# A decoder step on one Trainium2 core: the scan's first product, inverse and value transposes and the norms' sums in whole 128x128 tiles

## The chip, the core and the metric

The kernel runs on one core of a Trainium2 chip. The core has a matrix engine (TensorE, PE in the profile; PEld is its weight load), a vector engine (DVE), a scalar engine (ACT), GpSimd (POOL) and an engine that issues transfers (SyncE, SP), each with its own instruction stream. The metric is the device time of one execution, in microseconds (us), median of several runs. Everything below is 32-bit floating point.

## The reference

Two decoder layers run on 512 prompt tokens and 8 x 4 sample tokens, which share the weights (544 token columns in all). Cut to what matters here:

```
mod = silu(c) @ w_ada + b_ada                    # six vectors of 1024 per layer
h = rmsnorm(x, g) * (1 + mod[1]) + mod[0]
z = h @ w_in                                     # columns for four mixers and the merge gates
# A: causal pooling, windows 2/4/8/16    B: retention    C: short gated convolution    D: RWKV-7
def rwkv7_scan(r, w, k, v, a_vec, b_vec, S0):    # 4 heads, 64 x 64 state each
    def step(S, inp):
        rt, wt, kt, vt, at, bt = inp
        S = (S * wt[:, :, None, :]
             + jnp.einsum('bhij,bhj->bhi', S, at)[..., None] * bt[:, :, None, :]
             + vt[..., :, None] * kt[..., None, :])
        return S, jnp.einsum('bhij,bhj->bhi', S, rt)
...
mixed = jnp.sum(gates * proj, axis=2) @ w_out;   x = x + mod[2] * mixed
h2 = rmsnorm(x, g2) * (1 + mod[4]) + mod[3];     x = x + mod[5] * (W_down(silu(a) * b))  # [a|b] = dwconv3(h2 @ w_up)
```

with `rmsnorm(x) = x / sqrt(mean(x*x) + eps) * g`, and a last norm after both layers.

## The kernel before

**The weight stream.** Activations lie transposed: 128 channels on the partitions, tokens along the free axis, in two halves of 272 columns. The weights of each layer come as 138 units of 128x1024. `load_unit` brings a unit by a transfer on SP into one of three buffers named `raw` (the core's `in_wst`), ACT copies it rounded into `whi`, and DVE subtracts to get the rest, `wlo` (L110, L111). Each product then is three 128x128 by 128x272 matmuls, `mm3` (L130, L131, L132: hi by high part, hi by low part, lo by high part of the activations). There are 13,248 of them, called main matmuls below.

**The side work.** All else (the adaLN products `ada`, norms, the four mixers) is written as Python generators. After each `mm3`, `slot()` steps those whose due count of main matmuls has come; `yield 12` means twelve main matmuls later, a negative number that the step has nothing for PE. So PE's instruction order is fixed by the program text. The other engines' order comes from a scheduler. An entry with a `slack` waits for another PE step to come due, until it is later than its slack. A plain 32-bit matmul is two instructions in the trace (x8 in a row of the profile is four matmuls); the order listings count matmuls.

**The scan.** `rwkv` cuts the 512 tokens into 16 chunks of 32, with four heads indexed by (q, p), and then handles the 32 sample tokens. The inverse of each chunk's 32x32 triangle per head (`XT`) is worked out ahead. Per chunk three PE steps follow one another at 12, 12 and 18 main matmuls (`D_G`, `D_S`, `D_P`):

- G (L636): four products of 128 rows by 32 columns; ACT copies the result to `gs` (L639).
- S (L605): four products of a 32x32 inverse and a block of `gs`. DVE (L610) and ACT (L611) copy the result into `Z`, one copy each. At every second chunk `newZ` adds eight small transposes of values for the next two chunks (L593), which ACT copies into `Z` (L597).
- P and Y (L654, L658): four 64x64 and four 128x64 products; DVE adds and multiplies (L666, L672) to give the state rows of the next chunk's `Z`.

A chunk's three steps depend on one another through these copies. Where a copy is late, PE waits at the next step, and the main matmuls behind it wait too.

**The norms.** `rstd_of` gets a 128x272 tile of squares summed over the eight channel blocks. Four thin matmuls with a column of ones (L272) bring the sums to 68 partitions by 4; then ACT's square root (L274), DVE's reciprocal (L275) and DVE's spreading onto a diagonal (L279). Eighteen main matmuls later, a matmul with ones (L286) gives 128x272 again. It runs for both halves at four norms and the last, the first at the start for both halves together.

**adaLN.** `ada` for layer 0's four later vectors takes 32 steps of four matmuls (L220), each with a `raw` buffer and a 512 KB transfer of its own on SP (`in_wada`), and a pair of transposes per vector (L230); with slack 900.

**Pooling.** `DVE` does mixer A between scan steps: running sums (L1134 to L1141) and window differences (L1150 to L1153) over 64 or 128 rows of up to 678 columns.

Of the kernel before, what the change touches and what calls it, by code (L numbers as in the profile page):

```python
# [43 lines left out]
def tile_hybrid_step(ctx: ExitStack, tc: tile.TileContext, io: dict):  # L44
# [11 lines left out]
    t4p = ctx.enter_context(tc.tile_pool(name="t4p", bufs=13))  # L56
# [29 lines left out]
    V.memset(eps[:, 0:1], 1e-6 * 2.0 ** -20)  # L86
# [51 lines left out]

    nmm, gens = [0], []

    def spawn(g, after=0, slack=0):
        e = {"due": nmm[0] + abs(after), "pe": after >= 0, "g": g, "slack": slack}
        gens.append(e)
        return e

    def step(e):
        d = next(e["g"], None)
        if d is None:
            gens.remove(e)
        else:  # L150
            e["due"], e["pe"] = nmm[0] + abs(d), d >= 0

    def slot():
        for e in [e for e in gens if not e["pe"] and nmm[0] >= e["due"]]:
            step(e)
        if any(e["pe"] and nmm[0] >= e["due"] + e["slack"] for e in gens):
            for e in [e for e in gens if e["pe"] and nmm[0] >= e["due"]]:
                step(e)
# [106 lines left out]
    def rstd_of(accs, out):  # L265

        n = HALF // 4
        pm = PM()
        rt = ZR(400)
        m = 4 * len(accs)  # L270
        for i in range(m):
            PE.matmul(pm[0:n, i:i + 1], lhsT=accs[i // 4][:, n * (i % 4):n * (i % 4) + n], rhs=ones[:, 0:1], start=True, stop=True)  # L272
        r = rt[0:n, 300:300 + m]
        S.activation(r, pm[0:n, 0:m], AF.Sqrt, bias=eps[0:n, 0:1], scale=2.0 ** -20)  # L274
        V.reciprocal(r, r)  # L275
        ds = []
        for h in range(len(accs)):
            d = rt if h == 0 else ZR(HALF)
            V.tensor_tensor(out=d[0:n, 0:HALF].rearrange("p (i t) -> p i t", i=4),  # L279
                            in0=ident[0:n, 0:n].unsqueeze(1).broadcast_to([n, 4, n]),  # L280
                            in1=r[:, 4 * h:4 * h + 4].unsqueeze(2).broadcast_to([n, 4, n]), op=MUL)
            ds.append(d)
        yield 18
        for d in ds:
            ps = PM()
            PE.matmul(ps[:, 0:HALF], lhsT=ones[0:n, :], rhs=d[0:n, 0:HALF], start=True, stop=True)  # L286
            out.append(ps[:, 0:HALF])
# [11 lines left out]
    def norm_half(xt, half, acc, sA, shA, hh):  # L299
        c0, c1 = HS[half]  # L300
        rs = []
        yield from rstd_of([acc], rs)
        for k in range(8):
            u = ZR(HALF)
            V.tensor_tensor(out=u, in0=xk(xt, k)[:, c0:c1], in1=rs[0], op=MUL)
# [3 lines left out]
    def norm_final(xt, half, acc):  # L309
        c0, c1 = HS[half]  # L310
        rs = []
        yield from rstd_of([acc], rs)
        for k in range(8):
            x = xk(xt, k)[:, c0:c1]
            V.scalar_tensor_tensor(out=x, in0=x, scalar=pars[0][:, P_FG + k:P_FG + k + 1], in1=rs[0], op0=MUL, op1=MUL)
# [39 lines left out]
    def kv_rows(par):  # L355
        return slice(64, 128) if par == 0 else slice(0, 64)

# [18 lines left out]
    def rwkv(l, za, zb, M, yD):  # L376
# [51 lines left out]
        def products(T):  # L428
# [16 lines left out]
            for q in range(2):  # L445
# [5 lines left out]
                V.tensor_tensor(out=ot[:, :, :, 1:32], in0=kb[:, :, :, 1:32], in1=Er[:, :, :, 0:31], op=MUL)  # L451
                G.tensor_copy(ot[:, :, :, 0:32:st], kb[:, :, :, 0:32:st])
                V.tensor_tensor(out=ot[:, :, :, 32:64], in0=zb[r, 0:2, t0:t0 + n].rearrange("r p (c t) -> r p c t", t=32),
# [3 lines left out]
            for w, src in enumerate((kkb, za)):  # L457
                V.tensor_tensor(out=bkv[:, :, :, w, :], in0=src[:, 2:4, t0:t0 + n].rearrange("p q (c t) -> p q c t", t=32),
                                in1=Ei.rearrange("p q (c t) -> p q c t", t=32), op=MUL)
# [3 lines left out]
        yield 48  # L463
        for T in range(5):
# [29 lines left out]
            if T == 3:  # L494
                scr1 = drp.tile([64, 32, 32], F32, tag="scr1", name=nm("scr1"))
                for q in range(2):
                    r0 = 64 if q == 0 else 0
                    for p in range(2):
                        nc.sync.dma_start(scr1[(2 * q + p) * 16:(2 * q + p) * 16 + 16].rearrange("c s t -> s c t"),
                                          LG[q][r0:r0 + 32, 0:16, p, 0:32])  # L500
            if T < 4:
                yield 44
# [8 lines left out]
        for p in range(2):  # L511
            for q in range(2):
                r = par_rows(q)
                r0 = 64 if q == 0 else 0
# [1027 lines left out]
```

## Time and profile before

| | |
|---|---|
| three runs | 1969.99, 1971.23, 1971.52 us; median 1971.23 |
| profiled execution | 1970.54 us, span 1968.8 us, granted TensorE clock 0.997 |
| PE busy | 1924.9 us (98% of the span), 16868 instructions |
| PEld, DVE, ACT, POOL busy | 93%, 53%, 41%, 16% |
| transfers | 227.23 MB, mean 115 GB/s |

The profile is of one execution; the time of that execution exceeds its span by 1.7 us. Its page gives busy time per engine, the chain of work that ended last, and groups of instructions by line. A timeline lists instructions by start and length; a number in square brackets is the time for which the engine had been idle before, with what released it. Matmuls are pipelined, so the length of one (0.29 us for a main matmul) is longer than the distance between the starts of two.

### The profile page before, as it was taken

The numbers are of one execution on the slowest core, as the hardware profiler recorded it, in microseconds if no ns is written. First come the engines' busy times: TensorE is split into PE (matmuls) and PEld (weight loads), VectorE is DVE, ScalarE is ACT, GpSimd is POOL, SyncE is SP. The second block draws the span as 40 slices with busy tenths as digits, with TensorE's granted clock in tenths as the row PEclk, the third lists the DMA queues.
The fourth block names the chain that finished last, engine by engine and source line by source line (L and its number), as shares of the span: only waits on it lengthen the run. The fifth ranks groups of instructions, "written<-read, shape, count | busy, mean of one in ns | idle before, by whom it ended". The sixth has DMA issues, their size and how long they took to land.

```text
span 1968.8 us, 40136 instructions
## 1 busy us (share of the span) xinstructions
PE 1924.9 (98%) x16868; PEld 1834.8 (93%) x16868; DVE 1046.1 (53%) x2017; ACT 814.8 (41%) x1531; POOL 313.3 (16%) x589
## 2 busy tenths in 40 slices
PE   5999999999999999999999999999999999999997
PEld 5989888899998889999999998889999999999997
DVE  4476443543465444555664765345335665455565
ACT  4642322452355442435445423325423555243541
POOL 1110123213000110112202101241210022011210
PEclk9999999999999999999999999999999999999999
DMA  7324333433346742222332231134224132222221
GB/s 312 98 89 130 116 111 132 161 113 96 122 147 246 305 176 87 89 93 87 119 111 87 64 110 58 63 108 122 82 78 161 52 108 86 86 87 94 89 95 47
DMA packets 75557, 227.23 MB, mean 115 GB/s; under 512 B 20208, under 2 KB 23072, under 8 KB 73584
## 3 DMA queue, kind: packets, MB, share of 16 engines
q1 hardware_dynamic: 69872, 210.43, 32.2%
q0 software_dynamic: 3536, 11.53, 1.7%
q10 hardware_dynamic: 1968, 2.69, 0.5%
q8 instruction: 133, 2.18, 0.4%
q14 instruction: 48, 0.39, 0.1%
HBM read 213.33 MB, written 9.06 MB: 113 GB/s over the span
## 4 chain that ended last, share of the span: by engine, by line
PE 91%; DVE 4%; ACT 2%; DMA 2%; issue 1%; ACTq 0%; POOL 0%; DVEq 0%; POOLq 0%
PE pd L130 28%; PE pd L132 27%; PE pd L131 26%; PE pm L220 2%; DMA raw<-in_wst 1%; ACT whi L110 1%; DVE wlo L111 1%; PE pm L654 1%; PE pm L636 1%; PE pm L605 1%; DMA zr<-zr 1%; PE pm L658 1%; PE pm L593 0%; PE pm L477 0%; PE pm L484 0%
## 5 line engine op out<-in xcount | busy, mean ns | idle before, releaser
L130 PE MATMUL pd<-t,whi 128*128 128x272 f32 x4200 | 1234.8, 294 | 3.2 <-ACT t L373 1.8
L132 PE MATMUL pd<-t,wlo 128*128 128x272 f32 x4200 | 1214.5, 289 | 0.0
L131 PE MATMUL pd<-t,whi 128*128 128x272 f32 x4200 | 1208.5, 288 | 1.0 <-DVE t L374 0.8
L130 PEld LDWEIGHTS pd<-t,whi 128*128 128x128 f32 x4200 | 790.3, 188 | 41.4 <-issue 25.7
L131 PEld LDWEIGHTS pd<-t,whi 128*128 128x128 f32 x4200 | 792.5, 189 | 2.7 <-DVE t L374 1.8
L132 PEld LDWEIGHTS pd<-t,wlo 128*128 128x128 f32 x4200 | 791.3, 188 | 0.0
L111 DVE TENSOR_TENSOR wlo<-raw,whi 128x1024 fp32r<-128x1024 f32 x262 | 324.6, 1239 | 319.6 <-ACT whi L110 319.2
L110 ACT CAST whi<-raw 128x1024 fp32r<-128x1024 f32 x264 | 276.6, 1049 | 429.9 <-PE pd L131 417.3
L1256 POOL COPY off<-zr 128x18 f32<-128x18 f32 x88 | 77.2, 878 | 556.8 <-ACT zr L1254 556.8
L342 DVE SCALAR_TENSOR_TENSOR t<-pd,mod,t 128x272 f32<-128x272 f32 (+1 forms) x160 | 77.0, 482 | 106.9 <-PE pd L132 106.8
L1093 DVE TENSOR_TENSOR zr<-pd,zr 128x272 f32<-128x272 f32 x96 | 41.2, 438 | 124.9 <-PE pd L132 124.7
L1254 ACT COPY zr<-pd 128x272 f32<-128x272 f32 (+2 forms) x264 | 72.7, 311 | 72.9 <-PE pd L132 72.9
L1108 ACT ACTIVATE zr<-pd 128x272 f32<-128x272 f32 x128 | 50.5, 394 | 105.6 <-PE pd L132 105.5
L1094 POOL TENSOR_TENSOR t<-t,zr 128x272 f32<-128x272 f32 x64 | 68.9, 1093 | 119.5 <-DVE zr L1093 119.4
L1023 DVE SCALAR_TENSOR_TENSOR zr<-zr,par,zr 128x560 f32<-128x560 f32 x92 | 73.5, 801 | 9.7 <-ACT zr L1022 9.7
L1022 ACT ACTIVATE zr<-zr,par 128x560 f32<-128x560 f32 x92 | 70.2, 765 | 17.1 <-DVE zr L1047 9.6
L1024 DVE SCALAR_TENSOR_TENSOR zr<-zr,par,zr 128x560 f32<-128x560 f32 x92 | 73.4, 801 | 2.8
L373 ACT CAST t<-zr 128x544 fp32r<-128x544 f32 (+1 forms) x96 | 49.1, 530 | 61.8 <-DVE zr L1267 61.5
L374 DVE TENSOR_TENSOR t<-zr,t 128x544 fp32r<-128x544 f32 (+1 forms) x96 | 54.1, 580 | 30.0 <-ACT t L373 29.0
L259 ACT ACTIVATE zr<-t 128x272 f32<-128x272 f32 (+1 forms) x72 | 32.0, 454 | 86.6 <-DVE t L342 55.9
L610 DVE COPY z<-pm 32x128 f32<-32x128 f32 x34 | 9.8, 289 | 69.7 <-PE pm L605 69.4
L262 DVE TENSOR_TENSOR zr<-zr,zr 128x272 f32<-128x272 f32 (+1 forms) x63 | 29.9, 475 | 20.0 <-ACT zr L259 19.3
(286 smaller groups left out, 1635.1 us busy)
## 6 DMA issues: line engine op xcount, KB each, us to landing
raw<-in_wst SPq DMA_DIRECT2D x276, 512.0 KB, 3.5
t<-in_wada SPq DMA_DIRECT2D x32, 1024.0 KB, 9.7
raw<-in_wada SPq DMA_DIRECT2D x32, 512.0 KB, 3.6
zr<-in_rope POOLq DMA_DIRECT2D x16, 272.0 KB, 3.8
t<-in_xT SPq DMA_DIRECT2D x4, 544.0 KB, 6.7
zr<-zr ACTq DMA_DIRECT2D x32, 68.0 KB, 3.2
t<-in_xT SPq DMA_DIRECT2D x2, 1088.0 KB, 6.8
xs<-t SPq DMA_DIRECT2D x2, 1088.0 KB, 4.6
```

Source lines behind the costliest of these rows:

```text
L110: S.copy(hi, raw)
L111: (G if (l, u) in ((0, 1), (0, 2)) else V).tensor_tensor(out=lo, in0=raw, in1=hi, op=SUB)
L130: PE.matmul(ps, lhsT=a, rhs=xh, start=first, stop=False)
L131: PE.matmul(ps, lhsT=a, rhs=xl, start=False, stop=False)
L132: PE.matmul(ps, lhsT=b, rhs=xh, start=False, stop=last)
L342: V.scalar_tensor_tensor(out=x[:, c0:c0 + npc], in0=ps[:, :npc], scalar=gate[:, m, 0:1], in1=x[:, c0:c0 + npc], op0=MUL, op1=ADD)
L1022: S.activation(cv, u[:, 0:560], AF.Copy, scale=wcol(0))
L1023: V.scalar_tensor_tensor(out=cv, in0=u[:, 1:561], scalar=wcol(1), in1=cv, op0=MUL, op1=ADD)
L1024: V.scalar_tensor_tensor(out=cv, in0=u[:, 2:562], scalar=wcol(2), in1=cv, op0=MUL, op1=ADD)
L1094: (V if last else G).tensor_tensor(out=a[:, c0:c1], in0=a[:, c0:c1], in1=gs, op=ADD)
L1254: pad_evac(lambda o, i, sl: S.copy(o, i), u, ps, half, 2)
L1256: G.tensor_copy(off[:, 22 * s + j], u[:, 512:562].rearrange("p (x t) -> p x t", t=2)[:, 0:25:3, :])
```

## The change

Four things change in the scan. G becomes two 128x128 by 128x128 products, of which only the diagonal blocks are used; four copies (two on ACT, two on DVE, `g_out`) stack them into `gs`, 128x64. The four inverses of a chunk lie as blocks on the diagonal of one 128x128 tile (`XT`, now taken from the pool of large tiles, which gets a fourteenth buffer), so S is one product; its result is copied by two copies on DVE and two on ACT. The values are transposed four chunks at a time by two whole transposes (`values`, L581), copied by ACT, and put into `Z` by eight 32x64 copies on DVE per two chunks (L593). Row and column orders of the heads' blocks are swapped to fit.

In the norms, one 128x272 matmul with a full tile of ones takes the place of the thin sums, the spreading and the second matmul; the square root and the reciprocal run on 128x272. The pause of 18 main matmuls between the two goes.

In the step order, `ada` for layer 0 has slack 60 and prefers to run where a step in small tiles runs ("`yield n, True`"), and all that remains of it is finished when layer 0's mixers end.

```diff
+        due = [e for e in gens if e["pe"] and nmm[0] >= e["due"]]
+        urgent = [e for e in due if not e["slack"]]
+        tiled = any(e["tile"] for e in urgent)
+        for e in due:
+            late = nmm[0] - e["due"]
+            if tiled or late >= (1 if urgent else 4) * e["slack"]:
                 step(e)
...
+    def rstd_of(accs):
+        out = []
+        for acc in accs:
             ps = PM()
-            PE.matmul(ps[:, 0:HALF], lhsT=ones[0:n, :], rhs=d[0:n, 0:HALF], start=True, stop=True)
-            out.append(ps[:, 0:HALF])
+            PE.matmul(ps[:, 0:HALF], lhsT=ones, rhs=acc, start=True, stop=True)
+            rs = ZR(HALF)
+            S.activation(rs, ps[:, 0:HALF], AF.Sqrt, bias=EPS6)
+            V.reciprocal(rs, rs)
+            out.append(rs)
+        return out
...
+        def values(t0):
+            psV = PM()
+            for p in range(2):
+                PE.transpose(psV[:, 128 * p:128 * p + 128], zb[:, 2 + p, t0:t0 + 128], ident)
+            vT = M["pool"].tile([128, 2, 2, 64], F32, tag="vt", name=nm("vt"), bufs=2)
+            S.copy(vT.rearrange("r p q i -> r (p q i)"), psV[:, 0:256])
+            return vT
...
+                    for c, (vT, j) in enumerate(blocks):
+                        V.tensor_copy(Z[q][k_rows(q, p), c, p, :], vT[32 * j:32 * j + 32, p, q, :])
...
+        def g_out(psG):
+            gs = M["pool"].tile([128, 64], F32, tag="gs", name=nm("gs"), bufs=2)
+            for q in range(2):
+                for p in range(2):
+                    r = g_rows(q, p)
+                    (V.tensor_copy if q else S.copy)(gs[r], psG[r, 128 * q + 64 * p:128 * q + 64 * p + 64])
...
-        def sa_of(xt, gs):
+        def sa_of(ch, gs, Zc):
             psS = PM()
-            for p in range(2):
-                for q in range(2):
-                    r0 = 64 if q == 0 else 0
-                    PE.matmul(psS[r0:r0 + 32, 64 * p:64 * p + 64], lhsT=xt(q, p), rhs=gs[32 * q:32 * q + 32, p, :],
-                              start=True, stop=True)
+            PE.matmul(psS[:, 0:64], lhsT=XT[:, ch, :], rhs=gs, start=True, stop=True)
+            for q in range(2):
+                for p in range(2):
+                    r = b_rows(q, p)
+                    (V.tensor_copy if q else S.copy)(Zc[q][r, p, :], psS[r, 0:64])
...
             psG = PM()
-            for p in range(2):
-                for q in range(2):
-                    PE.matmul(psG[32 * q:32 * q + 32, 64 * p:64 * p + 64], lhsT=LG[q][:, ch, p, 0:32],
-                              rhs=Z[q][:, c % 2, p, :], start=True, stop=True)
+            for q in range(2):
+                PE.matmul(psG[:, 128 * q:128 * q + 128], lhsT=cols(LG[q][:, ch]), rhs=cols(Z[q][:, c % 2]), start=True, stop=True)
...
-            spawn(ada_all(0, range(2, 6), 1), -30, 900)
+            ada0 = spawn(ada_all(0, range(2, 6), 1), -30, 60)
...
         gates(lambda: yB[0], False, True, [lambda: None, lambda: finish(rets)])
+        if l == 0:
+            finish(ada0)
```

Three places show how instructions move. In the listings `pd` is the accumulator of main products, `pm` that of side work, `gs` and `z` the scan's tiles, `raw` a weight buffer and `t` a large tile; a number after a name tells tiles apart.

PE, layer 1, a scan step S with new values; before:

```order
L132 MATMUL pd_14093<-t_1446_11224,wlo_13857 128x272
L605 MATMUL pm_14097<-gs_14059,xt_11713 32x64 x4
L593 MATMUL pm_14106<-cst,t_1534_11736 32x64 x8
L130 MATMUL pd_14093<-t_1446_11224,whi_13856 128x272
L131 MATMUL pd_14093<-t_1448_11226,whi_13856 128x272
```

and the next such step with transposes after the change:

```order
L131 MATMUL pd_14214<-t_1443_11227,wlo_13983 128x272
L606 MATMUL pm_14224<-gs_14189,t_1740_13540 128x64
L581 MATMUL pm_14230<-cst,t_1528_11731 128x128 x2
L129 MATMUL pd_14214<-t_1443_11227,whi_13982 128x272
L130 MATMUL pd_14214<-t_1445_11229,whi_13982 128x272
```

One whole product stands where four small ones stood. Two transposes serve four chunks, where eight served two; at the steps between, S stands alone.

SP, the end of layer 0's mixers (`in_xT` is the input brought again for the residual); before:

```order
L103 DMA raw_831_6032<-in_wst 128x1024
L103 DMA raw_840_6114<-in_wst 128x1024
L103 DMA raw_857_6230<-in_wst 128x1024
L1220 DMA t4_851_6222<-in_xT 128x2176
L1220 DMA t4_852_6223<-in_xT 128x2176
L103 DMA raw_860_6236<-in_wst 128x1024
L103 DMA raw_863_6242<-in_wst 128x1024
L103 DMA raw_866_6248<-in_wst 128x1024
```

and after:

```order
L102 DMA raw_827_6029<-in_wst 128x1024
L102 DMA raw_836_6111<-in_wst 128x1024
L249 DMA raw_840_6134<-in_wada 128x1024
L1221 DMA t4_856_6271<-in_xT 128x2176
L1221 DMA t4_857_6272<-in_xT 128x2176
L249 DMA raw_848_6225<-in_wada 128x1024
L249 DMA raw_849_6231<-in_wada 128x1024
L249 DMA raw_850_6237<-in_wada 128x1024
L249 DMA raw_851_6243<-in_wada 128x1024
L249 DMA raw_852_6249<-in_wada 128x1024
L249 DMA raw_853_6255<-in_wada 128x1024
L102 DMA raw_862_6279<-in_wst 128x1024
```

Seven adaLN loads stand in a row at this point, through the three buffers `raw`. On PE their seven steps (`L225`) and two transposes stand back to back between the last main matmul of the mixers' output products and the next one. Before, these steps were spread over the main matmuls that follow.

DVE, layer 1, the first place where pooling meets a scan chunk; before:

```order
L1134 TENSOR_TENSOR t_1798_13860<-t_1798_13860 128x678
L610 COPY z_13704<-pm_13998 32x128
L1135 TENSOR_TENSOR t_1798_13860<-t_1798_13860 64x676
L1150 SCALAR_TENSOR_TENSOR zr_13970<-t_1798_13860,cst 64x512
L1151 SCALAR_TENSOR_TENSOR zr_13970<-t_1798_13860,cst 64x32
L1152 TENSOR_TENSOR zr_13970<-t_1798_13860,cst 64x15
L1150 SCALAR_TENSOR_TENSOR zr_13970<-t_1798_13860,cst 64x512
L1153 TENSOR_TENSOR zr_13970<-zr_13970,t_1798_13860 64x15
L1151 SCALAR_TENSOR_TENSOR zr_13970<-t_1798_13860,cst 64x32
L1152 TENSOR_TENSOR zr_13970<-t_1798_13860,cst 64x15
L666 TENSOR_TENSOR pt_14026<-pm_14017,pn_13933 128x128
```

and after:

```order
L1133 TENSOR_TENSOR t_1794_13869<-t_1794_13869 128x678
L601 COPY gs_14002<-pm_13999 32x64
L1134 TENSOR_TENSOR t_1794_13869<-t_1794_13869 64x676
L1149 SCALAR_TENSOR_TENSOR zr_13971<-t_1794_13869,cst 64x512
L1150 SCALAR_TENSOR_TENSOR zr_13971<-t_1794_13869,cst 64x32
L1151 TENSOR_TENSOR zr_13971<-t_1794_13869,cst 64x15
L1149 SCALAR_TENSOR_TENSOR zr_13971<-t_1794_13869,cst 64x512
L1152 TENSOR_TENSOR zr_13971<-zr_13971,t_1794_13869 64x15
L1150 SCALAR_TENSOR_TENSOR zr_13971<-t_1794_13869,cst 64x32
L1151 TENSOR_TENSOR zr_13971<-t_1794_13869,cst 64x15
L601 COPY gs_14002<-pm_13999 32x64
```

Before, one copy fed the next PE step, and it stood ahead of most of the pooling work. After, the two copies that S needs stand on either side of eight pooling instructions. A second place in each layer does the same to the two copies into `Z` (L610) ahead of P and Y.

More of the change, by code (lines that the diff above doesn't have):

```diff
@@ L141, in spawn @@
     def spawn(g, after=0, slack=0):
-        e = {"due": nmm[0] + abs(after), "pe": after >= 0, "g": g, "slack": slack}
+        e = {"due": nmm[0] + abs(after), "pe": after >= 0, "g": g, "slack": slack, "tile": False}
         gens.append(e)
@@ L149, in step @@
             gens.remove(e)
-        else:
-            e["due"], e["pe"] = nmm[0] + abs(d), d >= 0
+            return
+        d, e["tile"] = d if isinstance(d, tuple) else (d, False)
+        e["due"], e["pe"] = nmm[0] + abs(d), d >= 0
     def slot():
@@ L541, in rwkv @@
         psN = PM()
[L542 removed]
         for q in range(2):
[L544 to L545 removed]
             for p in range(2):
[L547 to L548 removed]
+                rr = b_rows(q, p)
+                PE.matmul(psN[rr, 0:32], lhsT=An[rr], rhs=LG[q][rr, 16, p, a_cols(q)], start=True, stop=True)
         for p in range(2):
@@ L582, in newZ @@
+        def newZ(blocks):
             Z = [M["pool"].tile([128, 2, 2, 64], F32, tag=f"z{q}", name=nm("z"), bufs=2) for q in range(2)]
-            G.memset(Z[0][64:96], 0.0)
-            G.memset(Z[1][0:32], 0.0)
-            psV = PM()
-            for c in range(nch):
+            for q in range(2):
                 for p in range(2):
-                    cc = (c * 2 + p) * 64
-                    for q in range(2):
-                        r0 = 96 if q == 0 else 32
-                        r = par_rows(q)
-                        t0 = 32 * (c0 + c)
-                        PE.matmul(psV[r0:r0 + 32, cc:cc + 64], lhsT=zb[r, 2 + p, t0:t0 + 32], rhs=ident[r, 64 * q:64 * q + 64],
-                                  start=True, stop=True)
@@ L616, in rwkv @@
             for q in range(2):
-                r0 = 64 if q == 0 else 0
-                PE.matmul(psX[32 * q:32 * q + 32, 32 * p:32 * p + 32], lhsT=IA[r0:r0 + 32, 32 * p:32 * p + 32],
-                          rhs=I2[r0:r0 + 32, 32 * p:32 * p + 32], start=True, stop=True)
-        V.tensor_copy(XTs[0:64].rearrange("r p t -> r (p t)"), psX[0:64, 0:64])
-        Z = newZ(0, 2)
+                rr = b_rows(q, p)
+                PE.matmul(psX[g_rows(q, p), 0:32], lhsT=IA[rr], rhs=I2[rr], start=True, stop=True)
+        for p in range(2):
+            for q in range(2):
+                V.tensor_copy(XT[g_rows(q, p), 16, b_rows(q, p)], psX[g_rows(q, p), 0:32])
+        vT = values(0)
+        Z = newZ([(vT, 0), (vT, 1)])
         for q in range(2):
@@ L726, in rwkv @@
                 PE.matmul(psXs[p][par_rows(q), :], lhsT=BK[r, 16, p, :], rhs=Zxs[p][r], start=True, stop=True)
-        V.tensor_tensor(out=yv[:, :, SEQ:TOK], in0=pY, in1=g0s[:, :, 1, :], op=ADD)
+        for q in range(2):
+            r = par_rows(q)
+            V.tensor_tensor(out=yv[r, :, SEQ:TOK], in0=pY[r], in1=g0s[r, :, 1 - q, :], op=ADD)
         for p in range(2):
@@ L908, in tile_hybrid_step @@
     afs = [ada_first(k) for k in range(8)]
-    rss = []
-    rg = rstd_of([acc[:, c0:c1] for c0, c1 in HS], rss)
-    next(rg)
+    rss = rstd_of([acc[:, c0:c1] for c0, c1 in HS])
     next(afs[0])
-    next(rg, None)
     hh = new_hh()
```

164 lines of the change are left out of this document (67 added, 97 removed).

## The prediction

> **What bounds the kernel now.** I read the page first, then PE's timeline around each kind of scan step and norm, PE's groups by line, DVE's groups in the stretch of layer 0 where scan and pooling overlap, SP's timeline at the end of layer 0's mixers, and the last 10 us.
>
> ```profile
> span 1968.8 us, 40136 instructions
> PE 1924.9 (98%) x16868; PEld 1834.8 (93%) x16868; DVE 1046.1 (53%) x2017; ACT 814.8 (41%) x1531; POOL 313.3 (16%) x589
> PE 91%; DVE 4%; ACT 2%; DMA 2%; issue 1%; ACTq 0%; POOL 0%; DVEq 0%; POOLq 0%
> ```
>
> PE is busy for 98% of the span and carries 91% of the chain that ended last. So a microsecond of side work taken out of PE's stream is a microsecond of time, as long as nothing new makes PE wait. What one step of side work costs is read from the starts of the main matmuls around it.
>
> ```profile
> 1184.38 0.29 PE L132 MATMUL pd<-t,wlo 128*128 128x272 f32 x1
> 1184.59 0.42 PE L636 MATMUL pm<-z,t 128*32 128x64 f32 x8
> ...
> 1185.17 0.29 PE L131 MATMUL pd<-t,whi 128*128 128x272 f32 x1
> 1185.29 0.29 PE L132 MATMUL pd<-t,wlo 128*128 128x272 f32 x1
> ...
> 1186.42 0.29 PE L132 MATMUL pd<-t,wlo 128*128 128x272 f32 x1
> 1186.63 0.41 PE L605 MATMUL pm<-gs,xt 32*32 32x64 f32 x8
> 1186.98 0.64 PE L593 MATMUL pm<-cst,t 64*32 64x64 f32 x16
> ...
> 1187.78 0.29 PE L131 MATMUL pd<-t,whi 128*128 128x272 f32 x1
> ```
>
> Undisturbed main matmuls start about 0.126 us apart (1185.17 to 1186.42 is ten of them). From the last main start ahead of a step to the second one behind it would be two pitches, 0.252 us, without the step; what is over is its cost. G: 1185.17 - 1184.38 - 0.252 = 0.54 us. S with eight transposes: 1187.78 - 1186.42 - 0.252 = 1.11 us. Where S stands alone it costs 0.54 us like G; it has as many instructions, and their durations are nearly equal:
>
> ```profile
> L636 PE MATMUL pm<-z,t 128*32 128x64 f32 x256 | 14.1, 228 | 1.7 <-DVE z L672 1.6
> L605 PE MATMUL pm<-gs,xt 32*32 32x64 f32 x256 | 13.2, 220 | 0.0
> ```
>
> Of this 0.54 us only 8 x 0.04 us is spacing inside the step; the rest is its first instruction starting 0.21 us behind the last main one (0.13 between main ones) and the second main one starting 0.23 us behind the first.
>
> **Whole tiles.** The trace has whole 32-bit steps of 128x128 elsewhere:
>
> ```profile
> 644.02 0.29 PE L132 MATMUL pd<-t,wlo 128*128 128x272 f32 x1
> 644.14 0.60 PE L230 MATMUL pm<-cst,zr 128*128 128x128 f32 x4
> ...
> 644.71 0.29 PE L131 MATMUL pd<-t,whi 128*128 128x272 f32 x1
> ```
>
> Four instructions cost 0.69 - 0.252 = 0.44 us, 0.11 us each, with no added pause at the entry. I price the new S (two instructions) at 0.22, the new G (four) at 0.44, S with two transposes at 0.44.
>
> *Scan.* Before: over 34 S steps 18 x 0.54 + 14 x 1.11 + 2 x 0.88 (half as many transposes), and some 0.9 for the first transposes of each layer, 27.9 us. After: 34 x 0.22 and ten pairs of transposes at 0.23, 9.8 us. Gain 18.1. G: 32 x (0.54 - 0.44), with a little back at the sample step, gain 3.1. P and Y stay.
>
> The Trainium skill ("TensorE: Matmul & The Clock Gate", Part 3, section "Measured speedup vs the span model") says that tiles packed in the array cost one matmul plus about 4 ns for each further tile. By that, S before would cost little more than the whole product after, the scan's gain would nearly vanish, and the time would be that of the third rival below; the rows disagree, with 40 ns from instruction to instruction and 0.54 us for the step.
>
> *Norms.*
>
> ```profile
> 1559.34 0.29 PE L132 MATMUL pd<-t,wlo 128*128 128x272 f32 x1
> 1559.46 0.60 PE L272 MATMUL pm<-cst,zr 128*68 128x1 f32 x8
> ...
> 1560.13 0.29 PE L131 MATMUL pd<-t,whi 128*128 128x272 f32 x1
> ...
> 1562.14 0.29 PE L132 MATMUL pd<-t,wlo 128*128 128x272 f32 x1
> 1562.26 0.62 PE L286 MATMUL pm<-zr,cst 68*128 68x272 f32 x2
> ...
> 1562.85 0.28 PE L131 MATMUL pd<-t,whi 128*128 128x272 f32 x1
> ```
>
> 0.54 and 0.46 us undisturbed. Over the seven norm halves inside the main stream, with the waits that some meet, the two sum to 10.1 us. After, seven steps of the second kind alone: 3.2 us. Gain 6.9. The gains sum to 28.1.
>
> **What it adds.** *adaLN in another order.* Most of its 32 steps now ride with S, P or Y in place of G, and three more stand alone:
>
> ```profile
> 547.55 0.29 PE L132 MATMUL pd<-t,wlo 128*128 128x272 f32 x1
> 547.77 0.64 PE L220 MATMUL pm<-raw,sc 128*32 128x256 f32 x8
> ...
> 548.57 0.29 PE L131 MATMUL pd<-t,whi 128*128 128x272 f32 x1
> ```
>
> Alone 0.77 us. Riding with G one added about 0.45 before, since both are small tiles and share one entry and exit; riding with the 64-wide steps 0.57. By the new order, 18.5 us against 17.3: cost 1.2.
>
> *The finish at the end of layer 0's mixers.* Seven steps run back to back at 542 us.
>
> ```profile
> 552.58 2.56 SPq L244 DMA_DIRECT2D raw<-in_wada  x2
> ```
>
> ```profile
> raw<-in_wada SPq DMA_DIRECT2D x32, 512.0 KB, 3.6
> ```
>
> A 512 KB load lands 3.6 us after its issue (the second fence, from the page's list of transfers); two behind each other take SP 2.56 us, 1.28 each, and I take landings of queued loads as 1.4 us apart. Three of the seven buffers can be filled ahead; the other four are each asked for when a step frees one. I follow SP's queue (the two 1088 KB loads of `in_xT` stand among them): the last load lands about 9 us after the last main matmul, while the seven steps have 3.5 us of work. PE waits 5.9 us more than it works. Ends: all loads hidden, 0; the first load held back by the other transfers, 9.
>
> *Pooling between two copies.*
>
> ```profile
> 1212.15 0.86 DVE L1135 TENSOR_TENSOR t<-t 64x676 f32<-64x676 f32 x1
> ```
>
> ```profile
> L1150 DVE SCALAR_TENSOR_TENSOR zr<-t,cst 64x512 f32<-64x512 f32 x4 | 3.0, 748 | 0.1
> L1151 DVE SCALAR_TENSOR_TENSOR zr<-t,cst 64x32 f32<-64x32 f32 x4 | 1.0, 245 | 0.0
> L1152 DVE TENSOR_TENSOR zr<-t,cst 64x15 f32<-64x15 f32 x4 | 0.7, 166 | 0.0
> L610 DVE COPY z<-pm 32x128 f32<-32x128 f32 x16 | 4.6, 289 | 33.4 <-PE pm L605 33.3
> L111 DVE TENSOR_TENSOR wlo<-raw,whi 128x1024 fp32r<-128x1024 f32 x15 | 18.9, 1258 | 14.7 <-ACT whi L110 14.6
> ```
>
> In the order after, eight instructions stand between the two copies that S waits for: 0.86 + 2 x 0.75 + 2 x 0.25 + 3 x 0.17 = 3.4 us; with the two copies (under 0.29 each) 3.9. The next step is due 12 main matmuls later, 1.51 us; so PE waits about 2.5 us. Two such places per layer, 10.0 us. The same pooling work already cost some 3.6 us before, where the state update and single copies stood behind it; net 6.4. Ends: 0 if DVE gets ahead of its order's due times, 10.
>
> *The reciprocal on 272 columns.*
>
> ```profile
> 15.39 0.20 DVE L275 RECIPROCAL zr<-zr 68x8 f32<-68x8 f32 x1 [2.36 <-ACT zr L274]
> ...
> 1958.47 0.65 PE L272 MATMUL pm<-cst,zr 128*68 128x1 f32 x8 [1.82 <-DVE zr L262]
> 1959.22 0.26 ACT L274 ACTIVATE zr<-pm,eps 68x4 f32<-68x4 f32 x1 [1.28 <-PE pm L272]
> 1959.52 0.17 DVE L275 RECIPROCAL zr<-zr 68x4 f32<-68x4 f32 x1 [1.10 <-ACT zr L274]
> 1959.73 0.44 DVE L279 TENSOR_TENSOR zr<-cst,zr 68x272 f32<-68x272 f32 x1
> 1960.22 0.99 PE L286 MATMUL pm<-zr,cst 68*128 68x272 f32 x2 [1.09 <-DVE zr L279]
> 1961.25 3.36 DVE L315 SCALAR_TENSOR_TENSOR t<-t,par,pm 128x272 f32<-128x272 f32 x8 [1.09 <-PE pm L286]
> ```
>
> Eight columns take about 25 ns more than four, 6.2 ns per column, so 272 take about 1.85 us as an estimate. The lower bound is another 272-column instruction, 0.44. Before, the tail from L272 to L315 is 2.78 us: 0.75 for the sums, 0.30, 0.21, 0.49 and 1.03. After: 1.03 for the one matmul, about 0.5 for the square root, 1.85 + 0.05: 3.5, cost 0.8. At the boundary of the layers the same chain stands before main work that needs it; I put 1.3 there. Together 2.1, ends -1 and 4.
>
> The Trainium skill ("VectorE: DVE Perf Modes", "First, the fixed hardware budget") has the reciprocal as divide steps with a repeat count of 8; at its 0.96 GHz that would be an estimated 272 x 8.3 ns = 2.3 us, and 0.4 us more at the tail. The slope between 4 and 8 columns is a little below it.
>
> *More copies between steps.* Each of the 33 chunks has two links, G to S and S to P, and each link now needs DVE as well as ACT; before, G to S needed ACT alone. P and Y, which waited for DVE (L610), cost 0.93 us in the median and 1.10 in the mean over 28 steps, 4.7 us of waits in all, most of it beside pooling. I put 3 for the new ones; ends 0 and 6. The start I put at 0.
>
> **Sum.** -28.1 + 1.2 + 5.9 + 6.4 + 2.1 + 3.0 = -9.5 us. The profiled execution, 1970.54, would be 1961.0. It lies 0.7 us under the median, so I forecast 1961.7.
>
> **The rivals.**
>
> *The links decide (slower).* A link is the step's result (0.23 us), two copies (2 x 0.29) and the release of PE (0.06), 0.87 us of the 1.51 that 12 main matmuls give; behind a whole L111 (1.26) it is 2.13, and PE waits 0.6. If half of the 66 links met that, 20 us, 17 over what I put: 1979. Against it: L111 takes 18.9 us of the 137 us window from which its row comes, 14%, so few links meet it whole. For it: L111's inputs arrive with the same units that pace PE, so the meeting is not random. From 0.19 us per link on (12.5 / 66), the change gains nothing.
>
> *Finish and pooling are hidden (faster).* If the seven loads have landed when PE gets there, and DVE's pooling stays clear of the links, 5.9 + 6.4 come off: 1949.4. For it: pooling's place in DVE's queue says nothing on when it starts, and the lone loads are short. Against it: three `raw` buffers, seven loads.
>
> *Whole steps are no cheaper than small ones.* If the new S costs 0.54 as before and G too, what is left is the transposes (7.3) and the norms (6.9): 14.2 - 18.6 = +4.4, 1975.6. For it: no row shows a whole 64-column product between main matmuls. Against it: 0.44 for four instructions at L230, 0.46 for two 272-column ones at L286.
>
> **How the numbers follow.** The forecast case 0.60 (1955 to 1967, from the ends of single terms); finish and pooling hidden 0.18; links 0.11; whole steps no cheaper 0.07; anything else 0.04. A measurement of this kernel tells about 0.2%, 3.9 us: faster is below 1967.3, slower above 1975.2. Faster: nearly all of the first two and half of the rest, 0.78. Within: 0.12, from the upper edge of the first, half of the third rival, and weak links. Slower: 0.10. The range 1948 to 1972 reaches from the hidden case to the start of the links' case, and leaves out about 2 in 10: part of the links' and third cases above, and part of the hidden one below.
>
> **What the profile after would show.** The new S (L606) at 0.22 us between main starts, G (L639) at 0.44; if they are near 0.54, the third rival holds. PE idle of about 6 us before L225 near 540 us; none means the second. Idle before L606 and L659 (P) of 2 to 3 us at four places beside pooling, and small ones elsewhere; some 0.3 us at most links mean the first. L278, the reciprocal, at 1.85 us. What would make me wrong most simply is the finish: its loads stand in one queue with others, and I followed that queue by hand.

## The result, and the profile after

The changed kernel takes 1985.69 us in the median of six runs (1979.86 to 1990.91), against 1970.11 before on the same chip: 1.0077 times as long, with a 95% interval of 1.0053 to 1.0101. The forecast was 1961.7, between 1948 and 1972. The kernel is slower by 0.8%, and its executions lie 11 us apart, where those of the kernel before lie 2 apart. The profiled execution took 1981.39 us. Its page:

```profile
span 1979.3 us, 39216 instructions
PE 1908.6 (96%) x16188; PEld 1831.9 (93%) x16188; DVE 1111.1 (56%) x2267; ACT 822.2 (42%) x1574; POOL 322.6 (16%) x627
```

PE is busy for 16 us less than before, and the span is 10.5 us longer. So the work did shrink, and PE stood still more. What single steps cost is seen where nothing waits (PE's timeline, layer 0, first S and second G):

```profile
208.72 0.29 PE L131 MATMUL pd<-t,wlo 128*128 128x272 f32 x1
208.85 0.33 PE L606 MATMUL pm<-gs,t 128*128 128x64 f32 x2
...
209.20 0.29 PE L130 MATMUL pd<-t,whi 128*128 128x272 f32 x1
...
213.64 0.29 PE L131 MATMUL pd<-t,wlo 128*128 128x272 f32 x1
213.77 0.61 PE L639 MATMUL pm<-z,t 128*128 128x128 f32 x4
...
214.34 0.28 PE L130 MATMUL pd<-t,whi 128*128 128x272 f32 x1
```

By the prediction's reckoning S costs 0.23 us here and G 0.45. Both prices hold to 0.01 us.

Where the time went is seen from the distance between the starts of the same main matmul in the two kernels. In the last column stands the best kernel of the experiments (`e8_best`, told below; this one execution took 1947.95 us, 6 us less than that kernel's median):

| main matmuls | what lies there | changed - before | best - before |
|---|---|---|---|
| 0 to 1200 | start, adaLN, scan's first steps | -5.2 us | -4.6 |
| 1200 to 1300 | pooling meets the scan, layer 0 | +8.7 | -3.6 |
| 1300 to 3060 | rest of layer 0's mixers | -4.6 | -4.8 |
| 3060 to 3080 | end of layer 0's mixers | +12.2 | 0.0 |
| 3080 to 5000 | feed-forward with the adaLN left | -2.9 | +1.0 |
| 5000 to 6700 | feed-forward, layer boundary | +1.9 | +1.0 |
| 6700 to 7800 | layer 1 up to pooling | -3.0 | -3.0 |
| 7800 to 7900 | pooling meets the scan, layer 1 | +8.9 | -3.0 |
| 7900 to the last | rest of layer 1 | -5.3 | -6.0 |

Three rows, together 29.8 us, make the loss, and 5000 to 6700 adds 1.9; everywhere else the change gains. The first of the three on PE, with the long waits only:

```profile
228.44 0.61 PE L639 MATMUL pm<-z,t 128*128 128x128 f32 x4
234.42 0.66 PE L606 MATMUL pm<-gs,t 128*128 128x64 f32 x2 [3.88 <-DVE gs L601]
...
245.21 0.41 PE L606 MATMUL pm<-gs,t 128*128 128x64 f32 x2 [2.32 <-DVE gs L601]
...
249.91 0.32 PE L659 MATMUL pm<-z,t 64*64 64x64 f32 x2 [2.37 <-DVE z L610]
```

and DVE at the first wait:

```profile
228.45 1.22 DVE L110 TENSOR_TENSOR wlo<-raw,whi 128x1024 fp32r<-128x1024 f32 x1 [1.41 <-ACT whi L109]
229.59 0.96 DVE L1133 TENSOR_TENSOR t<-t 128x678 f32<-128x678 f32 x1
230.58 0.22 DVE L601 COPY gs<-pm 32x64 f32<-32x64 f32 x1
230.81 0.86 DVE L1134 TENSOR_TENSOR t<-t 64x676 f32<-64x676 f32 x1
...
234.05 0.23 DVE L601 COPY gs<-pm 32x64 f32<-32x64 f32 x1
```

The block between the two copies takes 3.2 us, near the 3.4 of the prediction. Ahead of the first copy stand a whole `wlo` and another pooling instruction, 2.1 us. Now the granted clock, in stretches of this place (PE, PEld, DVE, ACT, POOL busy; then the clock, the share of DMA and GB/s):

```profile
225.00:230.00 5.00, 5.00 (x51) 4.74 (x51) 2.74 (x6) 1.91 (x5) 1.38 (x2) 1.00 0.09 34
230.00:234.00 4.00, 0.54 (x5) 0.32 (x3) 3.86 (x10) 0.00 (x0) 0.00 (x0) 1.00 0.41 131
234.00:237.00 3.00, 2.58 (x11) 2.61 (x12) 0.85 (x5) 0.79 (x3) 0.00 (x0) 0.51 0.00 0
237.00:240.00 3.00, 3.00 (x33) 2.75 (x32) 1.60 (x7) 0.37 (x1) 1.12 (x5) 0.93 0.00 0
```

Behind the pause PE gets half its clock for 3.4 us. In that time main matmuls start 0.23 us apart, so such a stretch costs up to 1.7 us on top of the pause. Between the start and the tail the changed kernel has five such stretches, at 234, 251, 1026, 1224 and 1234 us, and a longer one of 10 us at 545; the kernel before has one, at 332. All of them start at whole multiples of 3.413 us from one another (234.03 and 251.10 lie five apart), and so it is in every trace below: they lie on a grid of windows of that length. The one at 545 is the finish of adaLN:

```profile
541.08 1.50 PE L225 MATMUL pm<-raw,sc 128*32 128x256 f32 x24
545.64 2.31 PE L225 MATMUL pm<-raw,sc 128*32 128x256 f32 x16 [3.05 <-DMA raw<-in_wada]
548.13 1.08 PE L225 MATMUL pm<-raw,sc 128*32 128x256 f32 x8 [0.19 <-DMA raw<-in_wada]
550.64 1.08 PE L225 MATMUL pm<-raw,sc 128*32 128x256 f32 x8 [1.43 <-DMA raw<-in_wada]
552.21 0.69 PE L235 MATMUL pm<-cst,zr 128*128 128x128 f32 x2 [0.49 <-ACT zr L231]
```

It waits 5.2 us. Its steps, 0.64 us at full clock, take 1.08.

### The profile page after: what moved, and what is told of

Read it like the earlier page. It is cut to its first block, busy times and chain, and to the rows that moved or that the text cites. A ratio compares the mean times of both kernels' runs of the same rounds, so it can differ in the third digit from the quotient of the medians.

```text
span 1979.3 us, 39216 instructions
## 1 busy us (share of the span) xinstructions
PE 1908.6 (96%) x16188; PEld 1831.9 (93%) x16188; DVE 1111.1 (56%) x2267; ACT 822.2 (42%) x1574; POOL 322.6 (16%) x627
## 5 line engine op out<-in xcount | busy, mean ns | idle before, releaser
L110 DVE TENSOR_TENSOR wlo<-raw,whi 128x1024 fp32r<-128x1024 f32 x262 | 325.1, 1241 | 294.7 <-ACT whi L109 293.1
L601 ACT COPY gs<-pm 32x64 f32<-32x64 f32 x68 | 13.7, 202 | 70.3 <-PE pm L639 68.2
```

What stands on the lines that cost most here:

```text
L110: (G if (l, u) in ((0, 1), (0, 2)) else V).tensor_tensor(out=lo, in0=raw, in1=hi, op=SUB)
```

## The experiments

Each is a change of the changed kernel unless another is named. Times are medians, ratios those to the kernel before on the same chip. The experiments ran on three chips, on which the kernel before took 1968.34 to 1969.64 us in the median; so differences of a few us between two runs are read by the ratios too.

**Without the finish.**

```diff
-        if l == 0:
-            finish(ada0)
```

> The changed kernel without the finish of layer 0's adaLN at the end of its mixers; the seven steps left then run in the feed-forward stage as in the kernel before. Theory 1 (pauses of PE, each of which also costs clock): the stretch from main matmul 3060 to 3080, 12.2 us longer in the changed kernel, falls back to its old length, the seven steps cost 0.45 to 0.77 us each elsewhere (3 to 5 us), the half-speed stretch of 545 to 554 us is gone; about 8 us under the changed kernel. Theory 2 (whole tiles use more of the array and the clock is throttled for that): half-speed stretches stay or move elsewhere, and only the wait of some 5 us goes.

1979.17 us, ratio 1.0050 (1.0037 to 1.0063): 6.5 us under the changed kernel, with intervals that overlap. The half-speed stretch at 545 is gone, and main matmuls 3060 to 3080 take as long as before the change. Of the scan's stretches three stay; the one at 251 is not there, one at 246 is, and two more stand at 270 (6.8 us) and 399. So the scan's stretches are not the finish's doing, and theory 2 is not yet out. The stretch at 246 follows this wait:

```profile
245.78 0.57 PE L606 MATMUL pm<-gs,t 128*128 128x64 f32 x2 [2.33 <-DVE gs L601]
```

In the changed kernel the same S waited as long (2.32 us, at 245.21) and no half speed followed; it followed P's wait (2.37, at 249.91). Against the main matmuls around it, the grid lies 1.1 us later here than in the changed kernel.

**All link copies on ACT.**

```diff
-                    (V.tensor_copy if q else S.copy)(gs[r], ...)
+                    S.copy(gs[r], ...)
...
-                    (V.tensor_copy if q else S.copy)(Zc[q][r, p, :], psS[r, 0:64])
+                    S.copy(Zc[q][r, p, :], psS[r, 0:64])
```

> The changed kernel with all four copies after G and all four after S on ACT, none on DVE, so that pooling on DVE no longer stands between them. Theory 1: the waits before S (15 us in the profiled execution) and before P and Y beside pooling go, and with them the half-speed stretches at 234, 251, 1224 and 1234 us (1.7 us each); 13 to 20 us under the changed kernel. Theory 2: the half-speed stretches stay in the scan; 10 us or less. Rival to both (ACT now makes the links late: four copies of 0.2 us behind a 1.05 us cast are 1.9 us against the 1.51 us between two steps): small waits of 0.3 to 0.6 us at many links, 5 us or less under the changed kernel.

1964.58 us, ratio 0.9972 (0.9962 to 0.9982): 21 us under, a little more than the upper end. PE's longest scan wait, with what it waited for, the us in total, how often and the longest; first in the changed kernel, then in this one:

```profile
PE pm L606 <- DVE gs L601: 15.0, 9, 3.9
```

```profile
PE pm L639 <- DVE z L677: 4.4, 4, 2.1
```

S no longer waits for a copy, and ACT does not make the links late: outside the pooling places an S costs 0.22 us as before. What is left is G waiting for the state update, which stands behind pooling on DVE. The four half-speed stretches in the scan are gone as well, with the same whole matmuls in PE's stream. That rules out theory 2. One stretch stands at 324 us, at the place where the kernel before has its own, at 332; what lies ahead of it is told below.

**The norms of before**, with `rstd_of` and its callers as in that kernel:

```diff
-            PE.matmul(ps[:, 0:HALF], lhsT=ones, rhs=acc, start=True, stop=True)
...
-            V.reciprocal(rs, rs)
+            PE.matmul(pm[0:n, i:i + 1], lhsT=accs[i // 4][:, n * (i % 4):n * (i % 4) + n], rhs=ones[:, 0:1], start=True, stop=True)
...
+        yield 18
```

> The changed kernel with the norms of the kernel before. Theory of the prediction (norms gain 6.9 us on PE and lose 2.1 at the tail and the layer boundary): 4 to 6 us slower than the changed kernel. With the clock (the pause of 2.9 us and the half-speed stretch at 1025 us come from the longer norm chain): 2 to 4 us slower. Rival (the long reciprocal costs more than the matmuls save): faster than the changed kernel.

1986.34 us, ratio 1.0086 (1.0072 to 1.0100): 0.7 us over the changed kernel, less than either figure and within its spread. It says little alone; the norms are tried again below where nothing else disturbs.

**No finish and copies on ACT**, by the first two edits together.

> The changed kernel without the finish and with all link copies on ACT. Theory 1: the two gains add, 21 to 28 us under the changed kernel, 1958 to 1964 us, faster than the kernel before, and the spread between executions, 11 us in the changed kernel, shrinks to 2 us since no pause is near the length at which the clock drops. Theory 2: 15 us or less, and half-speed stretches stay in the scan.

1957.78 us, ratio 0.9946 (0.9934 to 0.9959). The gains add: 6.5 and 21.1 apart, 27.9 together. This kernel is faster than both, and under the one with copies on ACT the finish's 6.8 us stand clear of the intervals. The spread shrank to 5 us, not to 2.

**Pooling handed out.** Copies on DVE and ACT as in the change, but each long pooling instruction as a step of its own, the short ones in threes behind a long one:

```diff
+        def pooling(p, u, b2, b4, mm):
+            V.tensor_tensor(out=b2[:, 1:679], in0=u[:, 1:679], in1=u[:, 0:678], op=ADD)
+            yield -7
...
-            mms.append(mm)
+            mms.append(mm)
+            pgs.append(spawn(pooling(p, u, b2, b4, mm), -1))
```

> The changed kernel with its copies as they are (two on DVE, two on ACT per link), but pooling's DVE instructions handed out one every 7 main matmuls rather than all at once. Theory 1 (a whole block of pooling between two copies makes the pause): the waits of 2.3 to 3.9 us before S and P at four places shrink to under 1 us, no half-speed stretch in the scan; 12 to 18 us under the changed kernel, so about what moving the copies to ACT gave (21). Rival (DVE's total load on the links, not the block, is what delays them): waits are only spread over more chunks; 6 us or less under the changed kernel.

1971.38 us, ratio 1.0010 (1.0002 to 1.0019): 14.3 us under, as theory 1 had it, though its waits did not all fall under 1 us. Both copies to `gs` now stand together. In each layer one S still waits 2.3 us; in layer 0 its copies stand behind a whole `wlo` and one pooling instruction. Three half-speed stretches are left in the scan.

**Useless work in the pauses.** The step order and all copies as in the change:

```diff
+        def warm(n):
+            ps = PM()
+            for _ in range(n):
+                PE.matmul(ps[:, 0:HALF], lhsT=ones, rhs=cst[:, 0:HALF], start=True, stop=True)
...
+            if ch in (3, 4):
+                warm(8 if ch == 3 else 4)
             sa_of(ch, gs, [Z[0][:, c % 2], Z[1][:, c % 2]])
...
+            if ch == 4:
+                warm(4)
             psP = PM()
```

> The changed kernel with useless 128x272 matmuls on PE just ahead of the three steps that wait longest: eight (3.7 us) before S of chunk 3, four (1.8 us) before S and four before P of chunk 4, in each layer; 14.6 us more work on PE in all, laid into waits of 4.1, 2.5 and 2.4 us. Theory 1 with the clock as a cost of its own (a pause lowers it, for 3.4 us): the waits are filled, nothing else moves, and the half-speed stretches at 234, 251, 1224 and 1234 us vanish: 4 to 7 us faster than the changed kernel although it does more. Rival (the half speed does not come from the pauses, or the pauses' ends move back with the added work): the same or up to 10 us slower, and the stretches stay.

1980.40 us, ratio 1.0057 (1.0043 to 1.0070): 5.3 us under the changed kernel with 14.6 us more work, but the intervals overlap and the two profiled executions lie only 1.0 apart. What the traces show is the place itself: over main matmuls 1200 to 1300 and 7800 to 7900 this execution is 2.9 and 1.7 us shorter than that of the changed kernel, 4.5 in all. The same stretches as above, in this kernel:

```profile
225.00:230.00 5.00, 5.00 (x52) 4.74 (x51) 2.19 (x7) 1.62 (x4) 0.56 (x2) 1.00 0.24 89
230.00:234.00 4.00, 4.00 (x25) 3.57 (x24) 3.91 (x8) 0.41 (x2) 0.82 (x1) 1.00 0.41 131
234.00:237.00 3.00, 2.79 (x19) 2.27 (x18) 1.79 (x8) 0.80 (x3) 0.00 (x0) 1.00 0.00 0
237.00:240.00 3.00, 3.00 (x34) 2.74 (x34) 1.97 (x9) 0.37 (x1) 1.19 (x5) 1.00 0.00 0
```

DVE does the same; PE has no pause, and the clock stays at 1.00. The four stretches at 234 to 1234 us are gone. So the clock is a cost of its own, and here it came from PE standing still.

That is not its only source. This trace has a stretch at 332 us, like the kernel before, where PE is busy all the time with the scan's last small products (kernel before):

```profile
329.55 2.04 PE L685 MATMUL pm<-t,zr 64*64 64x8 f32 x64
```

**Pauses of known length**, in the kernel before:

```diff
+        def pauses():
+            for k in (1, 2, 3, 4, 5, 6, 7, 8, 9, 10, 3, 5, 7, 6):
...
+                for _ in range(k):
+                    V.tensor_tensor(out=d, in0=d, in1=d, op=MAX)
...
+                yield 160
```

> The kernel before with fourteen pauses of PE in the feed-forward stage of layer 0, one every 160 main matmuls (20 us): a matmul, a copy, a chain of 1 to 10 DVE instructions of 0.3 to 0.44 us on its result, and a matmul that waits for them, so pauses of about 1 to 5 us. If only pauses near or over some 3 us lower the clock, the short ones cost their own length and the long ones their length and 1.7 us; if the clock follows the mean activity or the array's use, no single pause is followed by half speed; if any pause does it, all fourteen are.

2076.59 us, 107 us more than the kernel before; 62.4 us of it are PE's idle time in the pauses. With DVE's other work between, the fourteen pauses came out at 1.4 to 7.4 us between the starts of the two matmuls. Three of them on PE, the last and next starts, and the clock around:

```profile
707.25 0.62 PE L1209 MATMUL pm<-cst 128*128 128x272 f32 x2
711.01 1.27 PE L1215 MATMUL pm<-zr,cst 128*128 128x272 f32 x2 [3.14 <-DVE zr L1213]
...
738.80 0.62 PE L1209 MATMUL pm<-cst 128*128 128x272 f32 x2
742.48 0.73 PE L1215 MATMUL pm<-zr,cst 128*128 128x272 f32 x2 [3.06 <-DVE zr L1213]
...
943.07 0.62 PE L1209 MATMUL pm<-cst 128*128 128x272 f32 x2
945.66 1.09 PE L1215 MATMUL pm<-zr,cst 128*128 128x272 f32 x2 [1.96 <-DVE zr L1213]
```

```profile
710.00:717.00 7.00, 5.99 (x24) 5.76 (x25) 0.95 (x2) 1.06 (x2) 0.00 (x0) 0.53 0.00 0
...
743.00:750.00 7.00, 7.00 (x57) 5.37 (x57) 3.31 (x5) 3.43 (x7) 1.09 (x3) 1.00 0.21 77
...
945.00:950.00 5.00, 4.34 (x20) 4.12 (x21) 0.57 (x2) 0.39 (x1) 0.00 (x0) 0.66 0.13 53
```

A pause with 3.14 us idle was followed by half speed for 7 us; one with 3.06 us by none; one with 1.96 us by half speed for 3.4. The shortest (1.4 us) had none, and all from 3.78 us on had some. So neither of the sharp rules put forward (a length of some 3 us, or any pause) holds. Half speed comes in steps of 3.4 us, one, two or three of them, 23 behind the pauses, which at 1.7 us each are some 39 more of the 107 us.

By these traces, what decides is where a pause lies on the grid. The windows in which these three pauses lie (the one of 3.06 us lies in two):

```profile
706.94:710.36 3.42, 0.93 (x6) 0.50 (x5) 2.42 (x5) 0.00 (x0) 0.00 (x0) 1.00 0.26 105
737.66:741.08 3.42, 1.76 (x13) 1.33 (x11) 2.60 (x7) 0.65 (x1) 0.00 (x0) 1.00 0.44 143
741.08:744.49 3.41, 2.01 (x15) 1.72 (x19) 1.27 (x3) 0.24 (x1) 0.00 (x0) 1.00 0.02 5
942.46:945.88 3.42, 1.46 (x10) 1.03 (x9) 2.12 (x5) 0.00 (x0) 0.00 (x0) 1.00 0.49 153
```

PE was busy for 0.93 and 1.46 us in the two windows that half speed followed, and for 1.76 and 2.01 in the two that it did not. The same reckoning over all fourteen traces, between start and tail, for windows at full speed: half speed came in the next window behind all 46 in which PE was busy for less than 0.45 of the window, behind 5 of 22 between 0.45 and 0.53, behind none of 374 between 0.53 and 1, and of the 7261 without any idle time behind only 8, all filled with the scan's last small products. So in this kernel a pause lowers the clock when it takes about half of one such window, 1.6 to 1.9 us; a pause of 3 us that two windows share may cost no more than its length.

**The best kernel**: the edits of no finish, copies on ACT and pooling handed out, together.

> The changed kernel without the finish, with all link copies on ACT and pooling handed out one instruction every 7 main matmuls. Theory 1: the two pauses of 1.9 and 2.4 us before G that were left (DVE's state update behind pooling) go with their half-speed stretch, 5 to 8 us under the kernel without finish and with copies on ACT: 1950 to 1953 us. Rival (DVE's load): no gain on that kernel, 1957 to 1959 us.

1953.93 us, ratio 0.9920 (0.9907 to 0.9933), 3.9 under the kernel without the third part, just short of theory 1's range. Its profiled execution, at 1947.95 the fastest of six, has no half-speed stretch between the start and the tail. The wait before G fell from 4.3 us in four to 0.6 in two.

**The norms, again**: the edit of the norms of before, made to the best kernel.

> The best kernel so far (no finish, copies on ACT, pooling handed out) with the norms of the kernel before, so that the norms' part of the change is seen without other pauses. The prediction's sum (6.9 us gained on PE, 2.1 lost at the tail and the layer boundary): 5 us slower than the best kernel, 1958 to 1960 us. Rival (old norms inside the changed kernel cost only 0.7 us, so the long chain gives nearly everything back): within 2 us of it.

1954.93 us, ratio 0.9933 (0.9920 to 0.9947): over the best kernel by 1.0 us in the times and 2.6 by the ratios, and the intervals overlap. The profiled executions lie 6.3 apart, 2.9 without the two half-speed stretches that only this one has (at 1226 and 1288 us). That is nearer to the rival than to the sum: the norms' part of the change is worth some 1 to 3 us, not 5.

**Another root**, on the best kernel:

```diff
-            S.activation(rs, ps[:, 0:HALF], AF.Sqrt, bias=EPS6)
-            V.reciprocal(rs, rs)
+            S.activation(rs, ps[:, 0:HALF], AF.Ln, bias=EPS6)
+            S.activation(rs, rs, AF.Exp, scale=-0.5)
```

> The best kernel with exp(-0.5 ln(x)) on ACT in place of the square root on ACT and the reciprocal (1.85 us) on DVE in the norms. If the reciprocal is what the norms' chain costs: the tail shortens by about 1.3 us, the boundary's pause of 2.9 us shrinks by as much or more, 2 to 4 us under the best kernel. Rival (ACT has to load another table for each of them, or DVE is not what the boundary waits for): within 1 us, or slower.

1955.52 us, ratio 0.9928 (0.9916 to 0.9941): 1.6 us over the best, within the spread, so no gain. The end of its timeline shows why:

```profile
1943.88 1.28 ACT L277 ACT_TABLE_LOAD   x1 [1.34 <-PE pm L275]
1945.18 0.49 ACT L277 ACTIVATE zr<-pm,eps 128x272 f32<-128x272 f32 x1
1945.68 1.28 ACT L278 ACT_TABLE_LOAD   x1
1946.98 0.43 ACT L278 ACTIVATE zr<-zr 128x272 f32<-128x272 f32 x1
```

ACT loads a table of 1.28 us for each of the two. These two loads, 2.56 us, are more than the reciprocal's 1.85.

**The old order of adaLN**, on the best kernel:

```diff
-            if tiled or late >= (1 if urgent else 4) * e["slack"]:
-                step(e)
+        if any(e["pe"] and nmm[0] >= e["due"] + e["slack"] for e in gens):
+            for e in [e for e in gens if e["pe"] and nmm[0] >= e["due"]]:
+                step(e)
...
-            ada0 = spawn(ada_all(0, range(2, 6), 1), -30, 60)
+            ada0 = spawn(ada_all(0, range(2, 6), 1), -30, 900)
```

> The best kernel with the order of layer 0's adaLN steps as before the change (slack 900, riding with any step that comes due). By the prices of the prediction: steps that now ride with G, which is whole, lose their common entry (0.77 in place of 0.57 us with small tiles), about 3 us slower for 15 such steps, or less where they ride with P and Y. Rival (the order is worth nothing): within 1 us.

1955.19 us, ratio 0.9930 (0.9917 to 0.9942): 1.3 us over the best in the times, 2.0 by the ratios, which does not stand clear of the spread. The order is worth 2 us or nothing.

**The changed kernel once more**, with no edit.

> The changed kernel once more, for a second trace of it. If the clock's windows run free of the program, the same pauses must meet them at other phases: other half-speed stretches than in the first trace (or other lengths, in steps of 3.4 us), main matmuls otherwise at the same distances, and times that differ between executions by 1.7 us per stretch. If the spread has another cause, the stretches are the same and the difference lies elsewhere.

1987.22 us, ratio 1.0091 (1.0070 to 1.0112). This trace has the same stretches within 2 us of their places in the first, and one more during the start, where PE waits anyway. So it shows neither of the two: against the main matmuls of the scans the stretches lie only 0.3 to 0.5 us later than in the first trace, so the run hardly varied what it set out to vary. The trace of the kernel without the finish, with its 1.1 us in layer 0, did: there the stretch behind P's wait went, and one behind S's wait came. Over the ten executions of the changed kernel, the first six give the granted clock with the time: 0.988 to 0.992 where they took 1979.9 to 1981.6 us, 0.984 to 0.987 where they took 1989.8 to 1990.9. The spread goes with the clock. Which further stretches make an execution of this kernel long was not caught in a trace and stays open.

## Why the prediction was wrong

**Right:** the prices of whole steps. S 0.22 forecast and measured, G 0.44 and 0.44, S with two transposes 0.44 and 0.40, a norm's matmul 0.46 and 0.46 (medians of the undisturbed ones). The third rival (whole steps no cheaper) is out, and with it the time that the prediction drew from the Trainium skill ("TensorE: Matmul & The Clock Gate", Part 3, section "Measured speedup vs the span model"): on this kernel a whole S took 0.22 us where four packed products took 0.54. In the profiled execution of `e8_best`, where pooling and finish are out of the way and the clock stays up, PE's last main matmul starts 22.9 us earlier than before; the gross gain of the sum was 28.1.

**The term that failed first is pooling between two copies**: 10.0 us gross, 6.4 net. Measured against the best kernel over the same hundred main matmuls it is 12.3 us in layer 0 (8.7 + 3.6) and 11.9 in layer 1 (8.9 + 3.0), 24 in all. The mechanism was the one I named, and two steps of its working were not. I let the wait begin at the first copy; 2.1 us of other work (L110 and L1133) stood ahead of it, so S waited 3.9 us in place of 2.5. And I counted one wait for the second place of a layer, where S and P both wait, 2.3 and 2.4 us in layer 0, 2.3 and 1.1 in layer 1; the S there waits mainly for what stands ahead of its first copy, again a `wlo` and a pooling instruction, with only one more pooling instruction between its copies. The waits sum to 8.6 us in layer 0 and 7.3 in layer 1; the two half-speed stretches of each layer, 3.4 us, make up most of the rest.

**The term that was missing is the clock.** The profile before shows 0.997 for the whole execution, and one half-speed stretch at 332 us lay behind a scan step of many small matmuls; I read the former and didn't look for the latter. `e6_fill` prices it at some 4.5 us for the two pooling places alone. The Trainium skill ("TensorE: Matmul & The Clock Gate", Part 1, section "What's actually happening") says that the clock falls to half after an idle window of 3413 ns, and that these windows run free of the program. The traces agree with the length, 3.413 us, with the cost of 1.7 us for each, and with windows that run free of the program: the same S's wait of 2.3 us was followed by half speed in one trace and not in another. They do not agree that the whole window has to be idle: in `e7_dose` one with 1.46 us of PE's work was enough. By that section's rule taken alone, pauses that I put at 2.5 us would have cost only their length; by the runs a pause of 2 us or more can cost 1.7 us on top.

**The finish** was forecast at 5.9 us of waits, and 5.2 were measured. But its 3.5 us of work took some 6 at half clock, and the main matmuls of the next 2 us ran at half speed too: 12.2 us at the place. Without it, the same steps cost 3.9 us elsewhere (3080 to 5000 in the table), which leaves 8.3; the medians give 6.5, and 6.8 with the copies on ACT.

**The norms** were forecast to bring 4.8 net and brought some 1 to 3 (`e9`). The reciprocal took 1.85 us, as estimated from its slope of four and eight columns. I had counted 3.1 us of waits among the gains that are not the matmuls' own; they were DVE's and came back in another place:

```profile
1025.35 0.36 PE L129 MATMUL pd<-t,whi 128*128 128x272 f32 x1 [2.87 <-DVE zr L337]
```

At the layer boundary PE now waits for the residual, which stands in DVE's queue behind the next norm's multiplications; before the change PE waited 1.4 us there. The tail from the last main matmul to the end is as long as before, 12.3 us against 12.4:

```profile
1969.95 0.49 ACT L277 ACTIVATE zr<-pm,eps 128x272 f32<-128x272 f32 x1 [1.35 <-PE pm L275]
1970.47 1.85 DVE L278 RECIPROCAL zr<-zr 128x272 f32<-128x272 f32 x1 [1.40 <-ACT zr L277]
1972.36 3.39 DVE L306 SCALAR_TENSOR_TENSOR t<-t,par,zr 128x272 f32<-128x272 f32 x8
```

**The order of adaLN**, put at a cost of 1.2 us, showed none: on the best kernel the old order was no faster (`e11`).

**The first rival** (late links, 1979) came nearest in time, and its mechanism had a small part in it. Away from pooling, S costs 4.3 us more than its price in all, over eight of the 34 steps, near the 3.0 that I put for it. At all eight a whole `wlo` stands ahead of DVE's copies, as that rival has it, and PE waits up to 0.6 us, the rival's price:

```profile
1297.47 1.23 DVE L110 TENSOR_TENSOR wlo<-raw,whi 128x1024 fp32r<-128x1024 f32 x1 [0.61 <-ACT whi L109]
1298.73 0.46 DVE L601 COPY gs<-pm 32x64 f32<-32x64 f32 x2
1299.33 0.41 PE L606 MATMUL pm<-gs,t 128*128 128x64 f32 x2 [0.53 <-DVE gs L601]
```

But it met few links and not half of them. Against the sum, pooling is 14 us over its gross term, the norms 2 to 4 short, the finish some 2 over and the links 1: 19 to 21, and 20 were missing in the profiled execution.

## What to carry to other kernels

When a step is made cheaper on the bounding engine but its operands now come through more copies, look up where each copy stands in the other engine's queue, and start the reckoning at what stands ahead of the first one. On this kernel a pause of the matrix engine cost its length and, where it took half of a 3.4 us window or more, 1.7 us of clock; so a few pauses of 2 to 4 us can undo the gain of some seventy shortened steps. Look at the granted clock in stretches of a few microseconds, not over the span; and hand out long side work in single instructions. With that, the copies moved and the finish left out, this change went from 0.8% slower to 0.8% faster.

## What the runs showed of the hardware

- Half speed of PE in steps of 3.413 us, after 12 of 14 pauses of 1.4 to 7.4 us, and not by their length alone (1.96 us idle sufficed, 3.06 did not). The steps lie on a grid that is not tied to the program: half speed followed all 46 windows of the grid with PE busy for less than 0.45 of them, and none of 374 with 0.53 to just under 1.
- Half speed also behind windows without a pause, filled with 64 products of 64x64 by 8 columns and others as small (8 windows).
- Matmuls whose result nobody uses, laid into pauses, made the two places 4.5 us shorter.
- Exchange of ACT's functions: 1.28 us for a table in front of `Ln` and again in front of `Exp`.
- A reciprocal of 272 columns on DVE takes 1.85 us, against 0.44 for a product of two tiles of that size.
